# Row maxima of an 8192 x 8192 matrix: unequal tail loads, 64 adjacent rows per partition, one store

## The chip, the cores and the metric

The kernel runs on one core of one Trainium2 chip. The metric is the device time of the program in microseconds (us); a time shown is the median of several runs.

## The reference

For every row of a float32 matrix the largest absolute value is computed: 8192 rows of 8192 columns in (268.4 MB), 8192 numbers out (32 KB).

```python
def setup_inputs():
    rows = 8192
    cols = 8192
    return {"x": np.random.randn(rows, cols).astype(np.float32)}

def reference(x):
    return np.linalg.norm(x, ord=np.inf, axis=1)
```

## The kernel before

Each of the 128 partitions takes 64 whole rows of 32 KB, two at a time. Everything is loaded by SP (`nc.sync.dma_start`) and reduced by VectorE along the columns with `reduce_max` on absolute values (the helper `absmax`, L80, L81). Three buffers `t` of two rows per partition (64 KB and a pad of 16 numbers) take turns, so SP may be up to three tiles ahead of VectorE; a load into a buffer waits until the last reduction that reads the buffer is done. The framework also gives the DMAs eight completion semaphores in rotation; a DMA whose semaphore is still in use by the eighth DMA before it waits for that one.

The rows are divided into a bulk and a tail.

- Bulk (L83 to L90): 48 rows per partition, in six groups `a` of eight adjacent rows, each taken in four tiles `n` of two rows. Within a tile neighbouring partitions are 8 rows, 256 KB, apart in memory (`x_b`, L64). One DMA of 8 MiB loads a tile (L86), and one reduction makes two results per partition, kept in `r_bulk`. After the loop ACT issues one store of `r_bulk` (L91); in memory each partition has six pieces of 8 results, 32 B, that lie apart.
- Tail (L93 to L116): the remaining 16 rows per partition, adjacent, so partitions are 512 KB apart (`x_t`, L66). Each row is loaded in the pieces that `TAIL` (L17) lists for it: eight rows whole, five in halves, two in quarters, the last in 2048, 2048, 2048, 1024, 512 and 512 columns. The DMA is at L100. Each piece has a reduction of its own into `part`. Before the last piece is reduced, `part` is reduced to the results of the first 15 tail rows (L105) and ACT stores these (L106). The pieces of the last row are reduced into the pad behind the buffer's columns, so that the reduction of the last piece (L109) covers the 512 columns and the five earlier results at once. SP stores this last column of results (L117), 4 B per partition.

`start_first_load_early` (L25) moves the issue of the first load to the start of the program. The order on each engine is that of the program text.

Of the kernel before, what the change touches and what calls it, by code (L numbers as in the profile page):

```python
# [1 line left out]
logging.getLogger("concourse").setLevel(logging.ERROR)  # L3

# [1 line left out]

# [4 lines left out]

F32 = mybir.dt.float32
X = mybir.AxisListType.X

TAIL = (  # L17
    [[8192]] * 8
    + [[4096, 4096]] * 5
    + [[2048] * 4] * 2  # L20
    + [[2048, 2048, 2048, 1024, 512, 512]]
)


def start_first_load_early(nc):  # L25


    sp = mybir.EngineType.SP
    first, *rest = nc.main_func.blocks
    for block in rest:  # L30
        insts = block.instructions
        for i, ins in enumerate(insts):
            if ins.engine == sp and type(ins).__name__ == "InstDMACopy":
                assert not ins.sync_info.on_wait
                moved = insts[i]
                block.instructions = insts[:i] + insts[i + 1 :]
                head = first.instructions
                at = next(k for k, h in enumerate(head) if h.engine == sp)
                first.instructions = head[:at] + [moved] + head[at:]
                return  # L40


@with_exitstack
def kernel(
    ctx: ExitStack,
    tc: tile.TileContext,
    x: bass.AP,
    out: bass.AP,
    G: int = 4,
    B: int = 2,  # L50
    BUFS: int = 3,
):
    nc = tc.nc
    P = nc.NUM_PARTITIONS
    rows, cols = x.shape


    n_tail = len(TAIL)
    assert n_tail % B == 0
    n_bulk_rows = rows // P - n_tail  # L60
    assert n_bulk_rows % (G * B) == 0
    A = n_bulk_rows // (G * B)
    split = n_bulk_rows * P
    x_b = x[:split].rearrange("(a p n b) c -> a n p (b c)", p=P, a=A, n=G, b=B)  # L64
    out_b = out[:split].rearrange("(a p n b) -> p a (n b)", p=P, a=A, n=G, b=B)
    x_t = x[split:].rearrange("(p t b) c -> t p (b c)", p=P, b=B)  # L66
    out_t = out[split:].rearrange("(p t) -> p t", p=P)

    sbuf = ctx.enter_context(tc.tile_pool(name="sbuf", bufs=BUFS))
    outp = ctx.enter_context(tc.tile_pool(name="outp", bufs=1))  # L70

    k_last = len(TAIL[-1])
    r_bulk = outp.tile([P, A, G * B], F32)
    r_tail = outp.tile([P, n_tail], F32)
    r_fin = outp.tile([P, 1], F32)
    k_max = max(len(r) for r in TAIL[:-1])
    part = outp.tile([P, n_tail - 1, k_max], F32)
    nc.vector.memset(part[:], 0.0)  # L78

    def absmax(o, i):  # L80
        nc.vector.reduce_max(out=o, in_=i, axis=X, apply_absolute_value=True)  # L81

    for a in range(A):  # L83
        for n in range(G):
            t = sbuf.tile([P, B * cols + 16], F32, tag="t")
            nc.sync.dma_start(out=t[:, : B * cols], in_=x_b[a, n])  # L86
            absmax(
                r_bulk[:, a, n * B : (n + 1) * B],
                t[:, : B * cols].rearrange("p (b c) -> p b c", b=B),
            )  # L90
    nc.scalar.dma_start(out=out_b, in_=r_bulk[:])  # L91

    for i in range(0, n_tail, B):  # L93
        t = sbuf.tile([P, B * cols + 16], F32, tag="t")
        for j in range(B):
            r = i + j
            at = j * cols
            last = r == n_tail - 1
            for k, w in enumerate(TAIL[r]):
                nc.sync.dma_start(  # L100
                    out=t[:, at : at + w], in_=x_t[i // B][:, at : at + w]
                )
                if last and k == k_last - 1:

                    absmax(r_tail[:, : n_tail - 1], part[:])  # L105
                    nc.scalar.dma_start(  # L106
                        out=out_t[:, : n_tail - 1], in_=r_tail[:, : n_tail - 1]
                    )
                    absmax(r_fin[:], t[:, at : B * cols + k_last - 1])  # L109
                elif last:  # L110
                    absmax(
                        t[:, B * cols + k : B * cols + k + 1], t[:, at : at + w]
                    )
                else:
                    absmax(part[:, r, k : k + 1], t[:, at : at + w])
                at += w  # L116
    nc.sync.dma_start(out=out_t[:, n_tail - 1 :], in_=r_fin[:])  # L117
    nc.at_finalize(start_first_load_early)


# [1 line left out]
_INS = ['x']  # L122
_OUTS = [((8192,), 'float32')]


# [23 lines left out]
```

## Time and profile before

| | |
|---|---|
| Median of 8 runs | 629.21 us (629.12 to 629.28) |
| Profiled execution | 629.27 us |
| Its span, first to last instruction | 627.5 us |
| VectorE busy | 552.7 us, 88% |
| DMA, mean rate over the span | 428 GB/s |
| Bulk reduction, 128 x 16384 | 17.22 us each, 24 of them |
| Tail reductions, 8192 / 4096 / 2048 / 1024 / 512 columns | 8.68 / 4.41 / 2.28 / 1.21 / 0.68 us |
| Bulk load, issue to landing | 40.7 us (median; it queues behind earlier loads) |
| Store of `r_bulk`, issue to landing | 58.0 us |
| Store of `r_fin`, issue to landing | 1.5 us |

The profile is of one execution. Its rows group instructions by line, engine, operation and tile; a reduction's line is that of the helper, L81, so the groups are told apart by tile and shape. "Idle before" is the time in which the engine had nothing to do ahead of such an instruction, with what ended it. The chain of waits is followed back from the last instruction to what released each step. DVE is VectorE; SPq and ACTq are the queues of SP and ACT, which issue the DMAs. "q1" is SP's DMA queue and "q10" ACT's. Beside the instructions the trace holds a record of each DMA packet (start, duration, bytes) and each completion event.

### The profile page before, as it was taken

How to read it: one execution, taken by the hardware profiler on the slowest of the kernel's cores; microseconds unless marked ns; L12 is line 12 of the kernel's file. 1: busy time of each engine (PE TensorE's matmuls, PEld its weight loads, DVE VectorE, ACT ScalarE, POOL GpSimd, SP SyncE). 2: the span in 40 equal slices, each digit the busy share in tenths (PEclk: the TensorE clock that was granted, in tenths of full speed). 3: DMA queues.
4: the chain of work that ended last, by engine and by line, in shares of the span. 5: the costliest groups of instructions: out<-in, count | busy, mean ns of one | idle time of the engine just before them, and what ended most of it. 6: DMA issues, size and time to landing. Idle time of an engine off the chain costs nothing.

```text
span 627.5 us, 196 instructions
## 1 busy us (share of the span) xinstructions
DVE 552.7 (88%) x58; POOL 0.2 (0%) x4
## 2 busy tenths in 40 slices
DVE  0588988888988889888898888998889999999998
POOL 0000000000000000000000000000000000000000
DMA  9999999999999999999999999999999999999996
GB/s 401 468 401 464 405 460 409 455 414 451 418 451 418 451 418 451 418 451 418 451 418 451 418 451 418 451 418 451 418 424 428 429 425 435 429 430 429 425 425 269
DMA packets 9138, 268.49 MB, mean 428 GB/s; under 512 B 1968, under 2 KB 1968, under 8 KB 2352
## 3 DMA queue, kind: packets, MB, share of 16 engines
q1 hardware_dynamic: 8208, 268.44, 99.2%
q10 hardware_dynamic: 928, 0.03, 0.1%
q14 instruction: 2, 0.02, 0.0%
HBM read 268.44 MB, written 0.03 MB: 428 GB/s over the span
## 4 chain that ended last, share of the span: by engine, by line
DMA 64%; DVE 30%; another core or an unknown queue 4%; issue 1%; SPq 0%
DMA t<-in_x_dram 64%; DVE r_bulk L81 24%; DVE part L81 5%; DVE t L81 1%; SPq L100 0%; DVE r_fin L81 0%
## 5 line engine op out<-in xcount | busy, mean ns | idle before, releaser
L81 DVE TENSOR_REDUCE r_bulk<-t 128x2 f32<-128x16384 f32 x24 | 413.3, 17220 | 69.7 <-DMA t<-in_x_dram 69.7
L81 DVE TENSOR_REDUCE part<-t 128x1 f32<-128x4096 f32 (+2 forms) x26 | 130.0, 5067 | 1.4 <-DMA t<-in_x_dram 1.4
L81 DVE TENSOR_REDUCE t<-t 128x1 f32<-128x2048 f32 (+2 forms) x5 | 8.6, 1746 | 0.3 <-DMA t<-in_x_dram 0.2
L78 DVE MEMSET part<- 128x60 f32 x1 | 0.1, 108 | 0.8 <-PEq L133 0.8
L81 DVE TENSOR_REDUCE r_fin<-t 128x1 f32<-128x517 f32 x1 | 0.7, 692 | 0.0
L81 DVE TENSOR_REDUCE r_tail<-part 128x15 f32<-128x60 f32 x1 | 0.2, 216 | 0.0
L133 POOL MEMSET const-bfloat16-1.0<- 128x1 bf16 x1 | 0.1, 102 | 0.0
L133 POOL MEMSET const-uint8-127<- 128x1 uint8 x1 | 0.1, 102 | 0.0
L133 POOL MEMSET const-float32-1.0<- 128x1 f32 x1 | 0.1, 99 | 0.0
L133 POOL MEMSET const-float32-0.0<- 128x1 f32 x1 | 0.1, 98 | 0.2 <-issue 0.2
## 6 DMA issues: line engine op xcount, KB each, us to landing
t<-in_x_dram SPq DMA_DIRECT2D x8, 4096.0 KB, 37.0
t<-in_x_dram SPq DMA_DIRECT2D x10, 2048.0 KB, 30.4
t<-in_x_dram SPq DMA_DIRECT2D x11, 1024.0 KB, 24.6
t<-in_x_dram SPq DMA_DIRECT2D x1, 512.0 KB, 15.9
t<-in_x_dram SPq DMA_DIRECT2D x2, 256.0 KB, 13.2
t<-in_x_dram SPq DMA_DIRECT2D x24, 40.7
out_dram<-r_bulk ACTq DMA_DIRECT2D x1, 24.0 KB, 58.0
out_dram<-r_tail ACTq DMA_DIRECT2D x1, 7.5 KB, 5.6
```

Of the source, the lines that this page charges most:

```text
L78: nc.vector.memset(part[:], 0.0)
L81: nc.vector.reduce_max(out=o, in_=i, axis=X, apply_absolute_value=True)
L133: nc = _bacc.Bacc("TRN2", target_bir_lowering=False, num_devices=1)
```

## The change

All 64 rows of a partition are now adjacent in memory, so that partitions are 64 rows, 2 MB, apart everywhere (`x_v`). There is one result tile `res` of 64 numbers per partition, and one store of it at the very end, issued by SP: 256 B per partition, 32 KB in all. The two stores that ACT issued are gone. The bulk keeps 24 tiles of two rows, with the same load size and the same reduction.

The tail keeps 16 rows in eight tiles of two rows, but `TAIL` now lists, for each tile, the widths of its loads over the 16,384 columns of both rows. There are 31 loads instead of 32. Seven of them cross from the first row to the second; `segments` cuts such a load into one part for each row, and each part gets a reduction, so there are 38 of these instead of 32. Going by the list, the widths fall toward the end to 1024 columns, from one to the next by a factor near 0.88. The last row comes in seven pieces; its last reduction covers 1024 columns and six earlier results. The reduction of `part` to the other 15 results follows the last piece of the row before the last.

```diff
-TAIL = (
-    [[8192]] * 8
-    + [[4096, 4096]] * 5
-    + [[2048] * 4] * 2
-    + [[2048, 2048, 2048, 1024, 512, 512]]
-)
+TAIL = [
+    [2944, 13440],
+    [4096, 12288],
+    [11520, 4864],
+    [7680, 8704],
+    [6528, 3328, 6528],
+    [4864, 4096, 3328, 4096],
+    [3968, 3584, 3328, 2944, 2560],
+    [2432, 2176, 1920, 1664, 1536, 1280, 1152, 1024, 1152, 1024, 1024],
+]
+
+def segments(loads, cols):
+    out, at = [], 0
+    for i, w in enumerate(loads):
+        end = at + w
+        while at < end:
+            r = at // cols
+            to = min(end, (r + 1) * cols)
+            out.append((i, r, at - r * cols, to - at))
+            at = to
+    return out
...
-    x_b = x[:split].rearrange("(a p n b) c -> a n p (b c)", p=P, a=A, n=G, b=B)
-    out_b = out[:split].rearrange("(a p n b) -> p a (n b)", p=P, a=A, n=G, b=B)
-    x_t = x[split:].rearrange("(p t b) c -> t p (b c)", p=P, b=B)
-    out_t = out[split:].rearrange("(p t) -> p t", p=P)
+    x_v = x.rearrange("(p t b) c -> t p (b c)", p=P, b=B)
+    out_v = out.rearrange("(p t) -> p t", p=P)
...
-    for a in range(A):
-        for n in range(G):
-            t = sbuf.tile([P, B * cols + 16], F32, tag="t")
-            nc.sync.dma_start(out=t[:, : B * cols], in_=x_b[a, n])
-            absmax(
-                r_bulk[:, a, n * B : (n + 1) * B],
-                t[:, : B * cols].rearrange("p (b c) -> p b c", b=B),
+    for i in range(n_bulk):
+        t = sbuf.tile([P, W + PAD], F32, tag="t")
+        nc.sync.dma_start(out=t[:, :W], in_=x_v[i])
+        absmax(
+            res[:, i * B : (i + 1) * B],
+            t[:, :W].rearrange("p (b c) -> p b c", b=B),
+        )
+
+    seen = {}
+    for i, loads in enumerate(TAIL):
+        t = sbuf.tile([P, W + PAD], F32, tag="t")
+        todo = segs[i]
+        at = 0
+        for j, w in enumerate(loads):
+            nc.sync.dma_start(
+                out=t[:, at : at + w], in_=x_v[n_bulk + i][:, at : at + w]
             )
-    nc.scalar.dma_start(out=out_b, in_=r_bulk[:])
+            at += w
+            for _, b, c, n in [s for s in todo if s[0] == j]:
+                r = first + i * B + b
+                k = seen.get(r, 0)
+                seen[r] = k + 1
+                lo = b * cols + c
+                if r < last:
+                    absmax(part[:, r - first, k : k + 1], t[:, lo : lo + n])
+                    if r == last - 1 and k == count[r] - 1:
+                        absmax(res[:, first:last], part[:])
...
-                    absmax(r_tail[:, : n_tail - 1], part[:])
-                    nc.scalar.dma_start(
-                        out=out_t[:, : n_tail - 1], in_=r_tail[:, : n_tail - 1]
-                    )
-                    absmax(r_fin[:], t[:, at : B * cols + k_last - 1])
+                elif k < n_last - 1:
+                    absmax(t[:, W + k : W + k + 1], t[:, lo : lo + n])
+                else:
+                    absmax(res[:, last:], t[:, lo : W + n_last - 1])
...
-    nc.sync.dma_start(out=out_t[:, n_tail - 1 :], in_=r_fin[:])
+    nc.sync.dma_start(out=out_v, in_=res[:])
```

More of the change, by code (lines that the diff above doesn't have):

```diff
@@ L48 @@
     out: bass.AP,
-    G: int = 4,
     B: int = 2,
     BUFS: int = 3,
+    PAD: int = 16,
 ):
@@ L55 @@
     rows, cols = x.shape
[L58 to L63, printed above, removed]
-    x_b = x[:split].rearrange("(a p n b) c -> a n p (b c)", p=P, a=A, n=G, b=B)
-    out_b = out[:split].rearrange("(a p n b) -> p a (n b)", p=P, a=A, n=G, b=B)
-    x_t = x[split:].rearrange("(p t b) c -> t p (b c)", p=P, b=B)
-    out_t = out[split:].rearrange("(p t) -> p t", p=P)
+    W = B * cols
+    n_rows = rows // P
+    n_bulk = n_rows // B - len(TAIL)
+    first = n_bulk * B
+    last = n_rows - 1
+    x_v = x.rearrange("(p t b) c -> t p (b c)", p=P, b=B)
+    out_v = out.rearrange("(p t) -> p t", p=P)
     sbuf = ctx.enter_context(tc.tile_pool(name="sbuf", bufs=BUFS))
     outp = ctx.enter_context(tc.tile_pool(name="outp", bufs=1))
[L72 to L77, printed above, removed]
+    segs = [segments(loads, cols) for loads in TAIL]
+    count = {}
+    for i, s in enumerate(segs):
+        for _, r, _, _ in s:
+            r += first + i * B
+            count[r] = count.get(r, 0) + 1
+    n_last = count[last]
+    k_max = max(n for r, n in count.items() if r < last)
+    assert n_last - 1 <= PAD
+    res = outp.tile([P, n_rows], F32)
+    part = outp.tile([P, last - first, k_max], F32)
     nc.vector.memset(part[:], 0.0)
@@ L81, in absmax @@
         nc.vector.reduce_max(out=o, in_=i, axis=X, apply_absolute_value=True)
-    for a in range(A):
-        for n in range(G):
-            t = sbuf.tile([P, B * cols + 16], F32, tag="t")
-            nc.sync.dma_start(out=t[:, : B * cols], in_=x_b[a, n])
-            absmax(
-                r_bulk[:, a, n * B : (n + 1) * B],
-                t[:, : B * cols].rearrange("p (b c) -> p b c", b=B),
-            )
-    nc.scalar.dma_start(out=out_b, in_=r_bulk[:])
[L93 to L101, printed above, removed]
-                )
-                if last and k == k_last - 1:
-                    absmax(r_tail[:, : n_tail - 1], part[:])
-                    nc.scalar.dma_start(
-                        out=out_t[:, : n_tail - 1], in_=r_tail[:, : n_tail - 1]
-                    )
-                    absmax(r_fin[:], t[:, at : B * cols + k_last - 1])
[L110 to L113, printed above, removed]
-                else:
-                    absmax(part[:, r, k : k + 1], t[:, at : at + w])
-                at += w
```

## The prediction

> **What bounds the kernel now.** I read the page's busy shares and slices first, then the groups by shape, then the chain of waits in order of time and the stretches near the end.
>
> ```profile
> span 627.5 us, 196 instructions
> ...
> DVE 552.7 (88%) x58; POOL 0.2 (0%) x4
> ...
> DMA  9999999999999999999999999999999999999996
> GB/s 401 468 401 464 405 460 409 455 414 451 418 451 418 451 418 451 418 451 418 451 418 451 418 451 418 451 418 451 418 424 428 429 425 435 429 430 429 425 425 269
> ```
>
> The transfers fill every slice; the alternation of 401 and 468 is whole 64 KB packets falling on either side of a slice edge. VectorE is 88% busy, so it is second in line. In the packet records of the trace all 16 DMA engines have a packet in flight at every moment from 20 to 620 us, without a gap.
>
> ```profile
> core 0: us, DVE busy (x) POOL busy (x), PEclk, DMA share, GB/s
> ...
> 222.00:242.00 20.00, 17.86 (x2) 0.00 (x0) 1.00 1.00 433
> ...
> 545.00:565.00 20.00, 20.00 (x4) 0.00 (x0) 1.00 1.01 433
> ```
>
> The first of these stretches has partitions 256 KB apart (the bulk, eight adjacent rows of 32 KB each), the second 512 KB apart (the tail, sixteen rows). Both run at 433 GB/s. The packet records say the same more finely: packets of 65,536 B take 2418 ns (median), of 32,768 B 1213, of 16,384 B 611, of 8,192 B 309. The four lie on one line, 7.8 ns + bytes / 27.2 GB/s for one engine, although the first size is on the 256 KB pitch and the others on 512 KB. So before the change the pitch costs nothing that can be seen: the engines set the rate, not the memory.
>
> ```profile
> L81 DVE TENSOR_REDUCE r_bulk<-t 128x2 f32<-128x16384 f32 x24 | 413.3, 17220 | 69.7 <-DMA t<-in_x_dram 69.7
> L81 DVE TENSOR_REDUCE part<-t 128x1 f32<-128x8192 f32 x8 | 68.9, 8677 | 0.4 <-DMA t<-in_x_dram 0.4
> ...
> L81 DVE TENSOR_REDUCE t<-t 128x1 f32<-128x2048 f32 x3 | 6.8, 2282 | 0.3 <-DMA t<-in_x_dram 0.2
> ```
>
> A tile of 8 MiB lands every 19.33 us (466.71 less 22.03, the landings of the 24th and the first tile, over 23) and takes VectorE 17.22. By shape a reduction takes 0.147 us + 1.041 ns per column; two in a row overlap by about 0.08 us, so each further one occupies 0.063 us + 1.041 ns per column. A column costs the transfer 1.18 ns. The ratio is 0.88.
>
> ```profile
> 603.17 17.07 DMA t<-in_x_dram
> 620.24 0.02 issue
> 620.26 2.55 DVE t L81 x2
> 622.81 0.78 issue
> 623.59 0.69 DVE t L81
> 624.28 0.02 issue
> 624.30 0.69 DVE r_fin L81
> ```
>
> The transfer leads the chain to 620.24; then VectorE ends it. The last completion event of a load is at 622.76, but the last reduction starts at 624.30 and ends at 624.99, 2.23 us after the data are there: four reductions (2048, 1024, 512, 517 columns) have queued up. The 0.78 marked "issue" is no idleness: the 1024-column reduction begins at 622.46 and lasts 1.21. Then come the store (1.5 us from issue at 625.02 to landing) and the end of the program.
>
> **What the Trainium skill says.** "DMA: Bandwidth & Descriptors", section "Where 436 GB/s comes from": 16 ports give 435.2 GB/s. The trace agrees: 433 in a full stretch. The same page, section "Latency and other measured facts": copies between HBM tensors in tiles of 128 partitions by 16 KiB ran at 207 GB/s per direction with partitions 512 KiB apart, 164 at 2 MiB, 103 at 4 MiB, and 214 with a pitch padded by 4 KiB. The change goes to 2 MiB. The trace does not show the 3% that the page has at 512 KiB; no run here yet shows 2 MiB. "VectorE: DVE Perf Modes", section "The perf-mode tier table (the rule you actually need)": tensor_reduce has the 1x mode alone, which fits 1.041 ns per column here at every width. Unequal widths cannot change that price.
>
> **The change part by part.** The sum is made against the profiled execution, 629.27 us (span 627.5 and 1.8 around it), 0.06 above the median of 629.21.
>
> Start and bulk: the first load, the 24 bulk loads and the 24 reductions keep size, order and waits. Only the source address changes, partitions 2 MB instead of 256 KB apart. Its price is bounded below by nothing (no packet can beat the engine's own rate, which it already has) and above by the page's 214 to 164: 32 tiles of 19.33 us become 32 of 25.23, +189 us. I take nothing. My reasons: the page's tiles were read and written, these are only read; the pitch of 512 KB costs no nanosecond in this trace; and a partition's packet here is up to 64 KB of adjacent bytes, where the page had 16. The upper end stays in the range.
>
> The two result stores in the stream (L91, 768 packets of 32 B, and L106, 128 of 60 B) go. Their packets took 0.54 us per engine (48 x 9 ns + 8 x 11 + two completion writes of 9). That is the upper bound of what the loads win; the lower is nothing, since short packets overlap others. While L91's store went through, 4 MiB loads landed every 9.72 us against 9.67 for half a bulk tile; over six of them that is 0.3 or less. I take 0.2. Also gone is SP's 23.3 us wait at L100 for L91's store. It was covered by the loads already queued: no engine idled. So nothing is won there.
>
> Tail: 32 loads become 31, so 8 data packets per engine fewer, 8 x 7.8 = 0.06 us. Landings of the small loads run slightly ahead of the packet formula; with 5.1 ns instead of 7.8 per packet a tally of landings and reductions gives the old end as 624.94 (measured 624.99) and the last landing as 622.76, as measured. With the new widths the same tally gives last landing 622.51 (0.2 from the stores, the rest from the packets).
>
> VectorE in the tail: 32 reductions of load parts become 38, since seven loads span two rows; 6 x 0.063 = 0.4 us more. The tally has it idle only 0.05 us before the 12,288-column load and 0.7 before the 11,520 one, then busy throughout: from 519.1 on every landing finds it 0 to 6 us behind, the last eleven at most 0.4 and the last three 0.1, since each width is about 0.88 of the one before. So at the end there is no queue: the last reduction (1024 + 6 columns, 0.147 + 1.073 = 1.22 us) starts at 622.59 and ends at 623.81. Old end 624.94, new 623.81: a gain of 1.13 us. The cover is thin: if VectorE came late by d, the end comes late by d.
>
> SP's queue: 31 tail issues at 0.33 to 0.43 us each, in bursts of at most eleven, are 5 us of issuing, against buffers that are released at least 20 us ahead (tile 6 of the tail waits for tile 3's last reduction at 554, its data are due from 583). The eight completion semaphores in rotation leave seven later loads, 8 us, in the queue at the narrowest. Hidden.
>
> Final store: 128 rows of 256 B instead of 4 B, 32 KB. Eight packets per engine take about 8 x 17 instead of 8 x 9 ns: +0.07 us. Above, the larger write might take 0.4 longer to be confirmed; below, no gain, since the wait for confirmation stays. I take 0.1.
>
> Sum: -1.13 + 0.1 = -1.03, so 629.27 - 1.03 = 628.2 us. The case's own range is 627.7 to 628.8 (0.5 for the stores and confirmation, 0.6 for VectorE being late).
>
> **The rivals.**
> (1) The 2 MB pitch slows the reads: slower. One mechanism, in the bulk and the tail alike: the 16 engines read at addresses multiples of 2 MB apart and hinder each other in memory, so packets exceed 2418 ns. For it: the page's 164 of 214. Against it: the reasons above. The page's whole factor gives 629 + 189 = 817; half of it, if reads bear half of the loss, 722, which is the time I put to it. It decides from small values: 617 us of transfers need only 0.4%, 9 ns per packet, to eat the gain of 1.0 and 1.3 us more. VectorE's gap before each bulk reduction, 2.1 us now, would grow to 2.1 plus the loss per tile.
> (2) The stores' packets really held back the loads by 0.54, and the new store costs nothing more: 628.2 - 0.34 - 0.1 = 627.8 by the transfers, just faster. Against it: the landings during L91's store.
> (3) VectorE loses its cover in the tail: the row-spanning loads hold back 13,440, 12,288 and 11,520 columns until whole, and if VectorE idles 1.1 us more in the sum there, the gain is gone: 629.3, no change. For it: only some 0.1 us separates its backlog from the last landing. Against it: shorter landings only raise its backlog, and longer ones hit both.
>
> **How the numbers follow.** Chances: 0.45 for my forecast, 0.40 for (1), 0.08 for (2), 0.07 for (3). A measurement of this kernel can tell about 0.2%, 1.26 us, from no change. Faster by more than that means under 627.95: all of (2) and a fifth of my case, 0.17. Slower means (1) and a little of (3), 0.42. Within: 0.41. Under (1) I put a quarter of its chance below 650, a third between there and 740, the rest above, to 817; so a range from 627.5 to 740 leaves 0.16 out above and 0.03 below. It is wide because the pitch cannot be priced from this trace.
>
> **What would show it.** In the profile after: packets of 65,536 B still at 2418 ns, bulk tiles landing every 19.33 us and gaps of 2.1 us before bulk reductions (step one right; anything longer is (1)); no store before the last; last landing near 622.5 and last reduction ending about 1.25 us after it (the widths); the last store 1.5 to 1.7 us from issue to landing. The prediction is wrong if bulk tiles land slower, or if VectorE is more than 0.5 us behind the last landing.

## The result and the profile after

The changed kernel takes 675.12 us (median of 11 runs, 666.75 to 681.55) against 629.21 before: slower by a factor of 1.069, 95% interval 1.067 to 1.071. The ratio leaves out the runs more than 1.5% above the fastest, which for a kernel that scatters by 2% takes off the upper runs; so it lies below the quotient of the medians, 1.073. The forecast of 628.2 was wrong in sign. The time lies on the side of the rival of the 2 MB pitch, at 46 us of the 94 that it was given.

The profiled execution took 675.79 us, 46.5 more than that of before. Lines of its page:

```profile
span 674.0 us, 197 instructions
...
DVE 554.3 (82%) x64; POOL 0.2 (0%) x4
...
DMA  9999999999999999999999999999999999999994
GB/s 366 323 401 397 412 412 432 432 436 432 420 412 416 436 436 436 436 436 436 436 412 432 401 436 436 420 420 412 412 404 423 390 421 402 378 369 367 302 227 131
...
L102 DVE TENSOR_REDUCE res<-t 128x2 f32<-128x16384 f32 (+1 forms) x25 | 414.5, 16580 | 88.1 <-DMA t<-in_x_dram 88.0
```

The DMA row is as full as before, though less is moved: an engine counts as busy while a packet (one partition's piece of a load) is in flight, and packets now last longer. The rate is the row to read. It is low at the start, comes up to 436, sags a little, and falls at the end. The same by stretch, columns as in the prediction's table (the last is GB/s), after the change:

```profile
0.00:100.00 100.00, 59.88 (x5) 0.20 (x4) 1.00 1.00 387
240.00:320.00 80.00, 71.52 (x5) 0.00 (x0) 1.00 1.00 433
320.00:480.00 160.00, 140.06 (x9) 0.00 (x0) 1.00 1.00 426
480.00:580.00 100.00, 92.78 (x15) 0.00 (x0) 1.00 0.99 400
580.00:620.00 40.00, 35.40 (x10) 0.00 (x0) 1.00 0.99 372
```

Before the change, without the two stretches in the middle (433 GB/s in both):

```profile
0.00:100.00 100.00, 69.59 (x6) 0.20 (x4) 1.00 1.00 430
...
480.00:580.00 100.00, 99.61 (x16) 0.00 (x0) 1.00 1.01 431
580.00:620.00 40.00, 38.86 (x15) 0.00 (x0) 1.00 1.00 423
```

So the DMA engines can still run at their own rate with partitions 2 MB apart (433 from 240 to 320 us), but not at the start, not quite in the later bulk (426) and not in the tail. There VectorE now waits for small loads that used to be there in time, as in these two lines:

```profile
642.31 2.69 DVE L102 TENSOR_REDUCE part<-t 128x1 f32<-128x2432 f32 x1 [3.19 <-DMA t<-in_x_dram]
647.99 2.42 DVE L102 TENSOR_REDUCE part<-t 128x1 f32<-128x2176 f32 x1 [3.00 <-DMA t<-in_x_dram]
```

Where the 46.5 us lie follows from the landings (the trace's completion events):

| | before | after | difference |
|---|---|---|---|
| 1st bulk tile lands at | 22.03 | 26.82 | +4.8 |
| 2nd, 3rd, 4th tile, after the one before | 19.3, 19.4, 19.4 | 22.9, 21.9, 20.2 | +3.7, +2.5, +0.9 |
| 24th bulk tile lands at | 466.71 | 485.04 | +18.3 |
| from there to the last landing | 156.05 | 185.35 | +29.3 |
| last landing to end of last reduction | 2.23 | 1.32 | -0.9 |
| from there to the end of the span | 2.5 | 2.3 | -0.2 |

The losses are 18.3 us up to the 24th tile and 29.3 after it; the first two rows are part of the 18.3 (11.8 of them by the fourth tile). The last two rows are gains, the first of them the one forecast for the widths. Another number is new: how far apart the 16 engines finish one load. Before, the first and the last engine's completion of a load are 0.7 to 0.9 us apart throughout. After, they are 1.9 apart for the first tile, 5.2 for the twelfth, up to 13.4 in the tail and 9.9 for the very last load.

### The profile page after: what moved, and what is told of

Read it like the earlier page. It is cut to its first block, busy times and chain, and to the rows that moved or that the text cites. A ratio compares the mean times of both kernels' runs of the same rounds, so it can differ in the third digit from the quotient of the medians.

```text
span 674.0 us, 197 instructions
## 1 busy us (share of the span) xinstructions
DVE 554.3 (82%) x64; POOL 0.2 (0%) x4
## 2 busy tenths in 40 slices
DMA packets 8066, 268.49 MB, mean 398 GB/s; under 512 B 1024, under 2 KB 1024, under 8 KB 2176
## 4 chain that ended last, share of the span: by engine, by line
DMA 73%; DVE 26%; another core or an unknown queue 1%; issue 0%; SPq 0%
DMA t<-in_x_dram 73%; DVE res L102 23%; DVE part L102 3%; DVE t L102 0%; SPq L118 0%
## 5 line engine op out<-in xcount | busy, mean ns | idle before, releaser
L102 DVE TENSOR_REDUCE res<-t 128x2 f32<-128x16384 f32 (+1 forms) x25 | 414.5, 16580 | 88.1 <-DMA t<-in_x_dram 88.0
L102 DVE TENSOR_REDUCE part<-t 128x1 f32<-128x8192 f32 (+18 forms) x31 | 131.4, 4277 | 24.0 <-DMA t<-in_x_dram 24.0
L102 DVE TENSOR_REDUCE t<-t 128x1 f32<-128x1152 f32 (+3 forms) x6 | 8.2, 1395 | 4.4 <-DMA t<-in_x_dram 4.4
```

## The experiments

Each kernel is compared with the kernel before on the same chip (629.17 to 629.53 us). Landings are from completion events, packet times from packet records. The pitch is the distance in memory between neighbouring partitions; the pitch theory says that the pitch of 2 MB causes the loss. The diffs are against the changed kernel, cut to the lines that matter; "..." marks what is left out.

**The parts apart.** Layout with the old widths:

```diff
-    [2944, 13440],
-    [4096, 12288],
...
+    [8192, 8192],
+    [8192, 8192],
+    [8192, 8192],
+    [8192, 8192],
+    [4096, 4096, 4096, 4096],
+    [4096, 4096, 4096, 4096],
+    [4096, 4096, 2048, 2048, 2048, 2048],
+    [2048, 2048, 2048, 2048, 2048, 2048, 2048, 1024, 512, 512],
...
```

> The layout (partitions 2 MB apart) and the single final store, with the tail loads of the kernel before (8192 down to 512 columns). Pitch theory: the loss stays, bulk packets of 65,536 B above 2418 ns on average, tail packets too; 655 to 685 us. Rival, that the unequal widths cause the slow tail: the bulk still loses some 18 us but the tail recovers its 156 us, about 648 us.

Measured: 662.72 us, ratio 1.054 (1.050 to 1.059). The 24th tile lands at 480.87 and the tail takes 176.6 us from there, 20.6 more than before. So most of the loss is there without the new widths, as the pitch theory has it. The widths are not innocent: 12 us separate this kernel from the changed one, 9 of them in the tail of the profiled runs.

The widths with the old layout and the old stores:

```diff
-    x_v = x.rearrange("(p t b) c -> t p (b c)", p=P, b=B)
+    x_b = x[:split].rearrange("(a p t b) c -> a t p (b c)", a=A, p=P, b=B)
+    x_t = x[split:].rearrange("(p t b) c -> t p (b c)", p=P, b=B)
+    x_v = [x_b[i // 4, i % 4] for i in range(n_bulk)] + [
+        x_t[i] for i in range(len(TAIL))
+    ]
...
+    nc.scalar.dma_start(out=out_b, in_=r_bulk[:].rearrange("p (a t) -> p a t", a=A))
...
```

> The unequal widths alone: partitions 256 KB apart in the bulk and 512 KB in the tail, and the three stores of before. Pitch theory: no loss, all packets at the engine's own rate, and the gain that the prediction gave to the widths, the last reduction ending 1.3 instead of 2.2 us after the last landing: 628.2 to 628.6 us. Rival, unequal widths cause the slow tail: 650 to 660 us.

Measured: 628.67 us, 0.6 under before, ratio 0.9992 (0.9984 to 1.0000). The rival falls: unequal widths cost nothing when partitions are 512 KB apart.

The changed kernel with the power of two taken out of the pitch, and nothing else:

```diff
-    x_v = x.rearrange("(p t b) c -> t p (b c)", p=P, b=B)
+    near = x[: P * (n_rows - 1)].rearrange("(p t) c -> p t c", p=P)
+    x_v = [near[:, i * B : (i + 1) * B] for i in range(n_rows // B - 1)]
+    x_v = [v.rearrange("p b c -> p (b c)") for v in x_v] + [
...
+    ]
```

> The changed kernel with partitions 63 rows (2,064,384 B) instead of 64 rows (2,097,152 B) apart, all loads, reductions and the store of the same size and order. Neighbouring partitions share a row, so some rows are reduced twice and the last 127 not at all. If the power of two in the pitch is what hurts: 628 to 629 us, all packets at 2418 ns. If any long distance between partitions hurts, or the widths or the final store do: about 670 us as in the changed kernel.

Measured: 628.53 us, ratio 0.9988 (0.9982 to 0.9995). This is the run that settles the cause. The loads have the same sizes, count, order and waits, and the distance is 1.6% shorter. In the page of this kernel the rate is that of before again, and so is VectorE's wait for the bulk (69.7 us before, 88.0 in the changed kernel):

```profile
GB/s 401 464 406 464 406 464 406 456 414 456 414 439 431 439 431 427 443 427 443 410 460 406 464 401 468 401 468 401 468 419 406 463 427 410 441 423 428 426 423 287
...
L108 DVE TENSOR_REDUCE res<-t 128x2 f32<-128x16384 f32 (+1 forms) x25 | 414.5, 16580 | 69.8 <-DMA t<-in_x_dram 69.8
```

The end of this kernel, in order of time, is the tail as the change meant it:

```profile
620.80 2.47 DVE L108 TENSOR_REDUCE t<-t 128x1 f32<-128x1152 f32 x2
623.31 1.23 DVE L108 TENSOR_REDUCE res<-t 128x1 f32<-128x1030 f32 x1
624.56 0.35 SPq L143 DMA_DIRECT2D out_dram<-res  x1
```

The last landing is at 623.02, the last reduction starts 0.3 later and ends 1.5 after the landing (2.23 before the change).

The widths and the single store, with partitions 256 KB apart everywhere:

```diff
-    x_v = x.rearrange("(p t b) c -> t p (b c)", p=P, b=B)
-    out_v = out.rearrange("(p t) -> p t", p=P)
+    x_g = x.rearrange("(a p t b) c -> a t p (b c)", a=H, p=P, b=B)
+    x_v = [x_g[i // (8 // B), i % (8 // B)] for i in range(n_rows // B)]
+    out_v = out.rearrange("(a p t) -> p a t", a=H, p=P)
...
```

> The unequal widths and the single final store, with partitions 256 KB apart everywhere (eight groups of eight adjacent rows); the store then has eight pieces of 32 B per partition, 1024 packets instead of 128. Pitch theory: no loss; the widths and the missing stores save 1.1 us and the store of 1024 pieces costs about 0.5 us more at the end, 628.3 to 629.0 us. Rival (widths): 650 to 660 us.

Measured: 629.32 us, ratio 1.0002 (0.9994 to 1.0010), a little above the expectation. The bulk is 0.7 us late in the profiled run, at its tenth and eleventh tile alone, and the tail not at all. The last store, 1024 pieces of 32 B with nothing left to hide it, takes 2.17 us from issue to landing, against 1.45 for 128 pieces of 256 B in the kernel of 63 rows.

**From which pitch, and in which stage.** 1 MB:

```diff
+    H = 2
+    x_g = x.rearrange("(a p t b) c -> a t p (b c)", a=H, p=P, b=B)
+    x_v = [x_g[i // 16, i % 16] for i in range(n_rows // B)]
...
```

> The changed kernel with two groups of 32 adjacent rows per partition, so that partitions are 1 MB apart; one final store, two pieces of 128 B per partition. If the loss sets in with the power of two gradually: some loss in the first tiles and in the short loads of the tail, 632 to 655 us. If 2 MB is the first pitch that hurts: 628 to 629 us.

Measured: 642.45 us, ratio 1.021 (1.019 to 1.022): half the distance still costs. But the place differs. The 24th tile lands at 481.63, 14.9 late; the tail then takes 156.4 us, as before the change.

```profile
0.00:40.00 40.00, 14.18 (x2) 0.20 (x4) 1.00 0.99 365
...
480.00:580.00 100.00, 97.44 (x17) 0.00 (x0) 1.00 1.00 431
580.00:620.00 40.00, 39.82 (x12) 0.00 (x0) 1.00 1.00 425
```

At 1 MB the start is nearly as slow as at 2 MB (the fourth tile lands at 90.03, against 91.87 in the changed kernel), while the short loads of the tail run at full rate: their 4,096 B packets take 159 ns. The part of the expectation that had the tail suffer at 1 MB was wrong.

Bulk at 2 MB, tail at 512 KB, and the reverse:

```diff
-    x_v = x.rearrange("(p t b) c -> t p (b c)", p=P, b=B)
+    x_b = x.rearrange("(p t b) c -> t p (b c)", p=P, b=B)
+    x_t = x[first * P :].rearrange("(p t b) c -> t p (b c)", p=P, b=B)
+    x_v = [x_b[i] for i in range(n_bulk)] + [x_t[i] for i in range(len(TAIL))]
```

> The changed kernel, its bulk 2 MB apart as it is, its tail 512 KB apart as before (the tail's rows come from the last quarter of the matrix, so some rows are reduced twice and some not at all). Pitch theory with two separate losses: the bulk keeps its 14 to 18 us, the tail loses nothing but the engines' spread at its end (some 3 us): 643 to 650 us. Rival, the tail's loss is a late effect of engines that the bulk has driven apart: about 670 us.

```diff
-    x_v = x.rearrange("(p t b) c -> t p (b c)", p=P, b=B)
+    x_b = x[: first * P].rearrange("(a p t b) c -> a t p (b c)", a=6, p=P, b=B)
+    x_t = x.rearrange("(p t b) c -> t p (b c)", p=P, b=B)
+    x_v = [x_b[i // 4, i % 4] for i in range(n_bulk)] + [
+        x_t[n_bulk + i] for i in range(len(TAIL))
+    ]
```

> The reverse: bulk 256 KB apart, tail 2 MB apart (again some rows twice and some not at all). Pitch theory with two separate losses: the bulk loses nothing, the tail its 29 us, and perhaps up to 10 more because the engines enter it abreast: 655 to 668 us. Rival, late effect of the bulk: about 629 us.

Measured: 638.05 (ratio 1.014, 1.012 to 1.016) and 652.10 us (1.037, 1.035 to 1.038), both a few us below the expectation. In the first the 24th tile is 10.5 late and the tail takes its 155.9 us; in the second the bulk is 0.5 late and the tail takes 179.6, 23.6 more. Two stretches of each, start and tail, the first kernel first:

```profile
0.00:100.00 100.00, 62.31 (x5) 0.20 (x4) 1.00 0.99 390
...
480.00:580.00 100.00, 99.38 (x17) 0.00 (x0) 1.00 1.00 430
```

```profile
0.00:100.00 100.00, 69.11 (x6) 0.20 (x4) 1.00 1.00 430
...
580.00:647.00 67.00, 50.11 (x23) 0.00 (x0) 1.00 0.97 300
```

Each stage loses by its own pitch, and 23.6 of the tail's 29.3 us are no late effect of the bulk; what makes up the other 5.7 was not tried. The bulk's loss differs from profile to profile with the same bulk (18.3 in the changed kernel, 14.2 with the old widths, 10.5 here).

**What the packet size does.** Every bulk tile in eight loads of 2048 columns, at 2 MB and at 63 rows:

```diff
-        nc.sync.dma_start(out=t[:, :W], in_=x_v[i])
+        for j in range(0, W, 2048):
+            nc.sync.dma_start(out=t[:, j : j + 2048], in_=x_v[i][:, j : j + 2048])
```

> The changed kernel with every bulk tile loaded in eight DMAs of 2048 columns, so packets of 8,192 B at the 2 MB pitch from the first tile on. Theory: short packets keep colliding; they took 486 ns on average in the tail of the run with the old widths, against 309 at 512 KB, so a bulk tile would land every 30 us instead of 19.5 and the whole take 850 to 950 us. Rival, that only the end of a kernel is slow (engines finishing apart): 670 to 690 us.

> The same loads of 2048 columns with partitions 63 rows apart (neighbours share a row; the last 127 rows are left out). Control: if it is pitch and packet size together, no packet is slow and the time is 630 to 642 us. If short loads are slow by themselves: as with 2 MB.

Measured: 960.12 us, 10 above the expected range, and 638.61 us, inside it (a single timing each). In the first a bulk tile lands every 32 us, where 30 were expected, in the second every 19.8. DMA row and rates of the first, then the rates of the second:

```profile
DMA  5899986699999999999999999999999999999997
GB/s 230 266 266 250 264 253 268 251 269 269 264 248 266 266 258 251 266 268 265 248 264 265 261 255 260 267 252 264 267 263 251 266 356 410 417 421 415 396 292 179
```

```profile
GB/s 387 425 428 424 422 428 427 421 424 427 426 422 425 428 425 420 427 428 421 423 427 427 422 424 428 424 422 425 427 426 458 429 426 420 439 428 429 425 423 279
```

With short packets 2 MB apart the stream does not recover in the 776 us of its bulk: 24 tiles of 8.39 MB in that time are 260 GB/s; then the longer loads of the first tail tiles come up to 421, and the last short ones fall again. So the slow end of the changed kernel belongs to its small loads, not to its being the end. The DMA row of the first kernel shows one thing more: in two slices, from 144 to 192 us, it falls to 6, and the packets take 309 ns in the median, no more than with 63 rows, but the rate is 268 and 251 as elsewhere. There the time is lost between packets instead of in them; why was not tried. Mean packet times over all these runs:

| bytes of a packet | 256 or 512 KB apart (before) | 2 MB apart | 63 rows apart |
|---|---|---|---|
| 65,536 | 2422 ns | 2502 (changed kernel) | 2423 |
| 32,768 | 1214 | 1232 (old widths) | |
| 16,384 | 612 | 644 (old widths) | 612 |
| 8,192 | 311 | 486 (old widths), 482 (short loads) | 311 |

From 16 to 8 KB the extra time of a packet goes from 5% to 56%. In the changed kernel the packets between these sizes and below are slow too: 13,312 B take 610 ns instead of 501 with 63 rows, 7,680 B 594 instead of 291. This fits the 12 us between the changed kernel and the old widths: loads under 4096 columns, packets under 16 KB, carry 42,368 of the tail's 131,072 columns in the new list and 24,576 in the old. It is no full account: about 3.4 us of the packets' extra time (4.6 against 1.2 per engine, from 480 to 560 us) lie where the tail starts, and long packets have part in it: those of 46,080 to 53,760 B take 126 to 173 ns more than with 63 rows. Which property of these loads does it was not tried.

**When the bulk recovers.** One buffer instead of three, at 2 MB and at 63 rows, so that the DMA engines run dry and start again for every tile:

```diff
-    BUFS: int = 3,
+    BUFS: int = 1,
...
```

> The changed kernel (2 MB apart) with one buffer instead of three: a load is issued only when the reductions of the tile before are done, so all 16 engines stop and start abreast for every tile. Only the comparison with the same kernel at 63 rows counts. Theory, a bulk tile is slow while the engines run abreast and recovers once they have drifted apart: every bulk tile is as slow as the first one of the changed kernel, 4 to 5 us over that of the 63 rows, so some 100 us more over the bulk. Rival, the first tiles are slow because the kernel has just begun: only the first three or four tiles are slower, 10 to 15 us over the bulk.

> One buffer with partitions 63 rows apart (neighbours share a row; the last 127 rows are left out). Control: every bulk tile takes about 38.5 us from landing to landing (17.2 of reduction, 19.3 of transfer, 2 of issue and completion), the whole about 1200 us; both theories expect that.

Measured: 1290.17 and 1185.95 us (a single timing each), 104 apart. A late stretch of each, VectorE's rows; the bracket holds the idle time before the reduction, which is the load:

```profile
871.77 17.22 DVE L102 TENSOR_REDUCE res<-t 128x2 f32<-128x16384 f32 x1 [26.04 <-DMA t<-in_x_dram]
913.65 17.22 DVE L102 TENSOR_REDUCE res<-t 128x2 f32<-128x16384 f32 x1 [24.66 <-DMA t<-in_x_dram]
955.99 17.22 DVE L102 TENSOR_REDUCE res<-t 128x2 f32<-128x16384 f32 x1 [25.11 <-DMA t<-in_x_dram]
```

```profile
806.29 17.22 DVE L108 TENSOR_REDUCE res<-t 128x2 f32<-128x16384 f32 x1 [22.04 <-DMA t<-in_x_dram]
846.02 17.22 DVE L108 TENSOR_REDUCE res<-t 128x2 f32<-128x16384 f32 x1 [22.52 <-DMA t<-in_x_dram]
885.33 17.22 DVE L108 TENSOR_REDUCE res<-t 128x2 f32<-128x16384 f32 x1 [22.08 <-DMA t<-in_x_dram]
```

At 900 us a 2 MB tile is still late. So is every one of the 24, by 3.0 us on average: landing to landing takes 41.5 to 43.3 us, against 39.0 to 39.7. The rival, that only a young kernel is slow, falls. That is less than the 4 to 5 expected; over the bulk it is 73 us, not 100 (the tail loses the other 31).

What recovers is thus a stream of large packets that is not broken off. In it one can see how far the engines are apart: 1.9 us growing to 5.2 in the changed kernel, 1.7 to 6.9 at 1 MB, while the rate comes up. With one buffer they stay 1.0 to 2.7 apart, with the short loads of the bulk 1.3 to 2.0, and there nothing recovers. So it would fit that engines at different places of their packets stay out of each other's way, and engines abreast do not. But this is not shown, and the distance alone does not set the rate. The last eight bulk tiles of the changed kernel are each 0.2 to 0.6 us late again with the engines 5.3 to 5.8 us apart, while in the kernel with the tail at 512 KB the last twelve bulk tiles land every 19.3 us at 4.0. And in the changed kernel's tail the engines come to be 13.4 us apart while the rate falls.

One buffer also shortens the queue: at most one tile is under way instead of three. The short loads of the bulk have no more under way (SP waits for a landing before 184 of their 192 issues) and lose 12 us a tile, so with the same bytes under way it is the short packets that lose more. Whether the pause or the shorter queue keeps the one buffer from recovering, and where the packets meet, was not tried.

**A kernel that keeps the idea.** 63 adjacent rows per partition and one row of the last 128, whose results are stored early:

```diff
+    n_adj = n_rows - 1
+    adj = x[: P * n_adj].rearrange("(p t) c -> p t c", p=P)
+    one = x[P * n_adj :]
...
+    out_one = out[P * n_adj :].rearrange("(p t) -> p t", t=1)
...
+            nc.sync.dma_start(out=t[:, :cols], in_=adj[:, 0])
+            nc.sync.dma_start(out=t[:, cols:W], in_=one)
+            absmax(res[:, 1:2], t[:, :cols])
+            absmax(r_one[:], t[:, cols:W])
+            nc.scalar.dma_start(out=out_one, in_=r_one[:])
...
```

> A complete kernel without the power of two: each partition holds 63 adjacent rows (2,064,384 B apart) and one row of the last 128; the first tile is loaded as two single rows, its odd result stored at once by ACT (4 B per partition), the other 63 results in one store at the end. If the exact power of two is all that hurts: 628.3 to 628.8 us, as with the pitch of 63 rows and just below the kernel before. Otherwise above 640 us.

Measured: 630.56 us, ratio 1.0020 (1.0013 to 1.0027), 2 us above the expectation. The pitch costs nothing here, but between 40 and 60 us twenty packets last 1.7 us per engine too long in sum, while the pieces of the early store are in the trace (35.5 to 55.1 us). The suspect was this store; the next run moves its 128 pieces of 4 B from adjacent places to places 252 B apart, and leaves the results of the first row out of the last store to make room. The diff is against the kernel above:

```diff
-    out_one = out[P * n_adj :].rearrange("(p t) -> p t", t=1)
+    out_one = out_v[:, :1]
...
-    nc.sync.dma_start(out=out_v, in_=res[:, 1:])
+    nc.sync.dma_start(out=out_v[:, 1:], in_=res[:, 2:])
```

> The kernel of 63 and 1 rows with its early store of 128 single results not to 512 adjacent bytes but to places 252 B apart (where the results of the first row belong, which are then not stored). That run stood still for 1.7 us per engine at 41 us, about when this store was in the queue. If its adjacent 4 B pieces are the cause: the standstill goes, 628.5 to 629.0 us. If the tile of odd rows or any small store causes it: 630.5 us as before.

Measured: 628.71 us, ratio 0.9991 (0.9984 to 0.9998). The standstill is gone (no extra packet time from 40 to 60 us), so the place to which the 4 B pieces went was its cause. That their lying side by side is what matters is the likely reading; other places were not tried.

The 48 rows of the bulk adjacent (1.5 MB), and the bulk in three groups of 16 (512 KB), each with the tail 512 KB apart, the bulk's results stored by ACT in the stream and the tail's by SP at the end:

```diff
+    x_b = x[:split].rearrange("(p t b) c -> t p (b c)", p=P, b=B)
+    x_t = x[split:].rearrange("(p t b) c -> t p (b c)", p=P, b=B)
...
+    nc.scalar.dma_start(out=out_b, in_=r_bulk[:])
...
+    nc.sync.dma_start(out=out_t, in_=r_tail[:])
```

> A complete kernel with the unequal widths: bulk of 48 adjacent rows per partition (1.5 MB apart), its results stored in one go by ACT after the bulk (192 B per partition), tail of 16 adjacent rows (512 KB apart) with one store at the end. If only powers of two from 1 MB up hurt: 628.1 to 628.6 us. If the distance itself or a multiple of 512 KB counts: like 1 MB, 635 to 645 us.

```diff
+    x_g = x[:split].rearrange("(a p t b) c -> a t p (b c)", a=3, p=P, b=B)
+    x_b = [x_g[i // 8, i % 8] for i in range(n_bulk)]
...
```

> A complete kernel for speed: unequal widths, bulk in three groups of 16 adjacent rows and tail of 16 adjacent rows (512 KB apart everywhere), the bulk's results stored by ACT in the stream (64 B pieces), the tail's 16 results by SP at the end. No pitch loss; 628.3 to 628.8 us, if short stores in the stream cost what the run with the widths alone shows.

Measured: 628.94 us, ratio 0.9994 (0.9986 to 1.0002), and 629.05, ratio 0.9992 (0.9983 to 1.0000). At 1.5 MB the first two tiles together are 0.7 us late and the rest is clean; at 512 KB everywhere nothing is lost. Both expectations were too low by some 0.3. So the results of every row can be had far below the time of the changed kernel: with the widths alone 0.60 us below the kernel before beside it, with 512 KB everywhere 0.48, with 48 and 16 rows 0.28. These are within the 0.2% that a measurement can hardly tell from no change, and which of them is best cannot be told.

## Why the prediction was wrong

**The failed step: the 2 MB pitch taken at nothing.** Under "Start and bulk" the prediction says "I take nothing" for the new source addresses, and its tally of the tail keeps the packet times of 512 KB. The pitch cost 18.3 us in the bulk and 29.3 in the tail of the profiled run. With 63 rows, and nothing else changed, both are gone.

Of the three reasons for nothing, that "these are only read" does not protect (all these runs only read, and lose). That "the pitch of 512 KB costs no nanosecond" was true, and stayed true with 512 KB everywhere, but it says nothing of the next doubling: 1 MB already costs 13 us in all. That a packet is "up to 64 KB of adjacent bytes" was half right: a stream of such packets comes back to 433 GB/s, one of 8 KB packets does not. In the changed kernel the loss is 7%, and not the 30% that the Trainium skill's ratio gave ("DMA: Bandwidth & Descriptors", section "Latency and other measured facts", 164 of 214 GB/s at 2 MiB). Where the whole bulk was made of 8 KB packets, 260 of 425 GB/s is lower than that ratio.

The tail, where the larger part of the loss lies, got no price of its own: the upper bound applied one factor to all 32 tiles alike. The prediction did not ask what happens to short packets, of which the change puts more at the end. Of the 29.3 us, 20.6 come with the old widths as well. Rival (1) had the sign and the cause, longer packets by the 2 MB pitch, in bulk and tail. That the engines hinder each other in memory, as it says, no run shows. It spread the loss evenly, but the middle of the bulk runs at 433 GB/s, and its 722 us doubled the loss.

**The widths: right mechanism, size too large.** With a harmless pitch the gain is 0.60 us (widths alone, at the edge of what can be told) to 0.74 (63 rows, one store) instead of 1.03. VectorE's queue at the end is all but gone: at 63 rows the last reduction starts 0.3 us after the last landing (0.1 forecast) and ends 1.5 after it, against 2.23 before. The mis-sized term is mainly the last landing: 623.02 instead of 622.51. The packet formula fitted to the old widths ran half a microsecond ahead of the new ones.

**The stores: consistent.** With the two stores in the stream the last landing was at 623.18, without them at 623.02: 0.16, where 0.2 was taken. It is one profile of each, and the pitch differs too, so this does not show the size. The final store of 256 B per partition takes 1.5 us to land, as the 4 B one did; 0.1 more was allowed.

**SP's waits, the reductions' prices, VectorE's cover in the tail: right.** At 63 rows the DMA share is 0.99 to 1.00 in every stretch, so no wait of SP reached the engines. VectorE's only notable idle time in the tail is the 0.6 us before the 11,520-column load (0.7 forecast).

**The chances** were 0.42 for slower and 0.41 for no change, so the doubt was stated, and only the single number stood on the reasons above. These argued from the absence of a loss at a smaller pitch.

## What to carry to other kernels

Before giving each partition a larger block of adjacent rows, look at the distance that it puts between partitions; here 1 and 2 MB cost 13 and 46 us, where the two stores saved were put at 0.2, and one row less (63 instead of 64) took the loss away. A DMA row of nines does not show it: look at the rate, and at how far apart the engines finish a load. An absent cost at one size is no evidence for the next size; short loads and restarts lost most here.

## What the runs showed of the hardware

- It is not the distance between partitions that costs: 2,064,384 B are free, 2,097,152 B 5% slower with the old widths and 7% with the new, 1,572,864 B 0.7 us late over the first two tiles, 1,048,576 B 2% slower, 524,288 B free. Of the distances tried, only the powers of two from 1 MB on lost more than 1 us.
- The loss changes along the stream: 64 KB packets at 2 MB start at some 350 GB/s and reach 433 after about eleven tiles, with the engines then finishing 5 us apart; a stream of 8 KB packets stays at 260, and a stream that starts anew for every tile stays 3.0 us late at each.
- 128 results of 4 B stored to 512 adjacent bytes held up the loads by 1.7 us per engine; the same results 252 B apart held up nothing that could be seen.
